# Second attention of a two-layer decoder: TensorE's order of rounds is pinned, the values products move to the third and fourth quarter, and gemm steps move to both ends

## The chip, the cores and the metric

The kernel runs on one core of one Trainium2 chip. The metric is the device time of one execution of the whole program, in microseconds; the times below are of several runs. One more execution was recorded by the hardware profiler, and every row of a trace shown here is from that one.

## What is computed

The reference is a decoder trunk of two layers on 512 tokens of 1024 channels, in float32. Each layer mixes tokens in two ways in parallel and then applies an MLP:

```python
h = rmsnorm(x, norm_mix)
proj = h @ w_in
q_a, k_a, v_a, f_a, q_b, kv_b, g_b, gate_a, gate_b = jnp.split(proj, ...)
...
o_a = fox_attention(...)                       # first attention: 8 heads, forget gate
y_a = from_heads(o_a) @ w_o_fox
...
o_c, o_s, o_w = nsa_attention(...)             # second attention: compressed, selected, window
o_n = g[..., 0:1] * o_c + g[..., 1:2] * o_s + g[..., 2:3] * o_w
y_b = from_heads(o_n.reshape(...)) @ w_o_nsa
mixed = jax.nn.sigmoid(gate_a) * y_a + jax.nn.sigmoid(gate_b) * y_b
x = x + mixed @ w_out
h = rmsnorm(x, norm_mlp)
x = x + jnp.square(jax.nn.relu(h @ w_up)) @ w_down
```

The second attention has 8 heads of 64 channels on 2 key and value heads. Its selected branch chooses up to 16 blocks of 64 keys; a sequence of 512 tokens has only 8, so that branch attends to all earlier tokens through its own keys and values. The window of 512 covers them too. Both branches are thus plain causal attention with keys of their own; the compressed branch has 31 pooled keys.

## The kernel before

**Products.** A float32 product is three matmuls on operands split into a high and a low half: `gemm` (L219 to L221) issues high weight by high input, high by low, low by high for each block of 128 channels. A weight tile arrives as `raw` by a DMA on SP's queue; `convert` makes the halves, `wh` by a cast on ScalarE (L189) and `wl` by a subtraction on VectorE (L190). One conversion covers one weight tile of 128 x 1024. A *gemm step* is what `gemm` issues between two `yield`s: two blocks, six matmuls of 512 columns into the PSUM bank `ps_mm`. A whole projection is four steps.

**The second attention.** It is `attend_pairs`, called once per layer with eight pairs. Pair 2p is the selected branch (kind 0) of heads 2p and 2p+1, pair 2p+1 the window branch of the same two heads. In round t the loop interleaves the scores of pair t, the values of pair t-1 and gemm steps; there are rounds 0 to 8, the last with values only. A round has four quarters. The tuples of the plan say how many steps of the scores and of the values generator go into each quarter.

- `pair_scores` takes the query rows in blocks of 128, last block first (i = 3, 2, 1, 0). For each it makes scores (L590) in one of two PSUM banks `ps_S`, the row maximum on VectorE (`softmax_part`, L542, output `mx`), the exponential on ScalarE (L543), and after every second block the normalised halves on ScalarE (L560) and VectorE (L561). Those go to SP's queue as a DMA that transposes them into PT (L611). Block 0 is made for a pair and its mate at once from the shared keys `kk`, so only pairs of kind 0 have it: a *kk pair*, two scores groups of 256 columns.
- `pair_values` multiplies PT with the values (L623) in five steps: three products on the blocks of rows 3 and 2, then two on the rest. At the last step of a window pair `after` adds the compressed branch (L1065) and makes the head outputs, `oh` on ScalarE (L1073) and `o` on VectorE (L1074).

**The gemm steps beside it.** The generator `fill2` hands out 88 steps: the gate projections (`gate_tanh`, L1096), the half products of the first attention's output with `wo` (`half`, summed by `ma`, L1106), the last two query projections, and beside two of these the compressed scores (`cmp_gen`): six matmuls (L792 to L794), a copy on ScalarE (L796), four transposes (L800), a softmax in small steps. `lead` steps go ahead of round 0, `NSA_FILL` are owed in each quarter of rounds 0 to 7, `LAST_FILL` in each quarter of round 8, and `run(fill)` issues what is left. Behind that come the half products of the second attention's output with `wo` and the weight tiles of the MLP, whose first sums on VectorE are at L1518 (from `raw` of `wup`) and whose halves ScalarE makes at L1536 (`sh`).

**What sets the order.** The code's order is what the program emits; a scheduler then orders each engine's instructions by its own estimate of when operands are there, as long as dependencies hold. `high_priority(20)` in `softmax_part` lets maxima and exponentials go ahead of what was emitted shortly before. The first attention ahead of it (`attend`) runs eight *fox* units in the same manner, with transposes on TensorE (L463).

Of the kernel before, what the change touches and what calls it, by code (L numbers as in the profile page):

```python
# [137 lines left out]
def run(*gens):  # L138
    for g in gens:
        for _ in g:  # L140
            pass


class Body:
# [469 lines left out]
    def pair_values(self, P):  # L614
# [22 lines left out]
        for w, (o, b) in enumerate(((X, 1), (Y, 3))):  # L637
            product(parts(o)[:, :, 128:], b, 8, slice(w, w + 1))
            if not first:
                P["after"](w)  # L640

    def attend_pairs(self, pairs, fill, rate, lead):

        n = len(pairs)
        owed = 0.0
        for _ in range(lead):
            next(fill)
        self.PP = self.EE.bitcast(F16).rearrange("p a (b k) -> p (a b) k", k=128)
        for t in range(n + 1):
            plan = []  # L650
            if t < n:
                while not pairs[t]["ready"]():
                    next(fill)
                plan.append((self.pair_scores(pairs[t]), (2, 2, 2, 2) if pairs[t]["kind"] == 0 else (2, 2, 2, 0)))
            if t:
                plan.append((self.pair_values(pairs[t - 1]), (0, 2, 1, 2)))
            for k in range(4):
                for g, at in plan:
                    for _ in range(at[k]):
                        next(g, None)  # L660
                if k == 3:
                    for g, _ in plan:
                        for _ in g:
                            raise AssertionError
                owed += rate if t < n else self.LAST_FILL
                while owed >= 1.0:
                    owed -= 1.0
                    next(fill, None)
        run(fill)

    def compress(self, kc, vc, small, l):
# [275 lines left out]
    def layer(self, l, u):  # L947
# [55 lines left out]
        def proj(i, key, fn, tag="mm"):  # L1003
            def done(ps):
                st[key] = fn(ps)
            return self.block(wb[i], u, done, tag)
# [27 lines left out]
        def qproj(p):  # L1034
            return proj(12 + p, ("qb", p), lambda ps: self.q_pair(self.roped(ps)))

        def cmp_gen(hk):
            yield from self.cmp_probs(hk)
# [19 lines left out]
        def nsa_pairs(p):  # L1058
            hk, f = divmod(p, 2)
            O = []  # L1060

            def after(side):
                ps, q = O[side], slice(256 * side, 256 * side + 256)
                for e in range(2):
                    nc.tensor.matmul(ps[:, 256 * e:256 * e + 256], self.vz[:, hk, e], self.pc[hk][f][:, q],  # L1065
                                     start=False, stop=True, skip_group_check=True)
                if side == 0:
                    st["ob", p] = self.t("tmp2", [128, T], name="o")
                o = st["ob", p]
                t = self.t("tmp", [128, 256], name="oh")  # L1070
                for e in range(2):
                    s, x, c = slice(64 * e, 64 * e + 64), slice(64 * (1 - e), 64 * (1 - e) + 64), slice(256 * e, 256 * e + 256)
                    nc.scalar.activation(t[s], ps[x, c], AF.Copy, scale=self.sc[x, 2:3])  # L1073
                    nc.vector.scalar_tensor_tensor(o[s, q], ps[s, c], self.sc[s, 2:3], t[s], op0=OP.mult, op1=OP.add)  # L1074
                if side == 1:
                    st["ob", p] = self.out_pair(o)

            q = lambda e: st["qb", p][:, e]
            gate = lambda br: lambda rows: gt[:, rows, br, 2 * p:2 * p + 2].rearrange("p b h -> p h b")
            b_ = dict(kind=1, ready=lambda: hk in self.pc, q=q, k=lambda: st["kw"][:, hk], O=O,  # L1080
                      v=lambda b: VN[:, b, 2 + hk], gate=gate(2), after=after)
            a_ = dict(kind=0, ready=lambda: ("qb", p) in st and "kw" in st, q=q, k=lambda: st["ks"][:, hk], O=O,
                      v=lambda b: VN[:, b, hk], gate=gate(1), mate=b_,
                      kk=lambda: self.kk[:, :, hk].rearrange("p f b t -> p f (b t)"))
            return [a_, b_]
# [8 lines left out]
        def gate_tanh(ps, tag="tmp"):  # L1094
            s = self.t(tag, [128, T], name="gate")
            nc.vector.tensor_mul(s, ps, R)  # L1096
            nc.scalar.activation(s, s, AF.Tanh, scale=0.5)
            return s

        def gated(m0):  # L1100
            for m in (m0, m0 + 1):
                yield from proj(16 + m, ("ga", m), gate_tanh)
            w = self.weights(a["wo"][l, 0, m0 // 2].rearrange("p i c -> p (i c)"))
            for m in (m0, m0 + 1):
                yield from half(0, m, w)
                nc.vector.scalar_tensor_tensor(MA[m // 2][:, m % 2], st["ga", m], 1.0, st["y"],  # L1106
                                               op0=OP.add, op1=OP.mult)

        def fill2():
            yield from beside(cmp_gen(0), gated(0))  # L1110
            yield from qproj(2)
            yield from gated(2)
            yield from qproj(3)
            yield from beside(cmp_gen(1), gated(4))
            yield from gated(6)
            for m in range(8):
                yield from proj(24 + m, ("gb", m), lambda ps: gate_tanh(ps, ("oh", "ol")[m % 2]))

        self.attend_pairs([u for p in range(4) for u in nsa_pairs(p)], fill2(), self.NSA_FILL, 2)
        yb = [st["ob", p] for p in range(4)]  # L1120


# [10 lines left out]
        for m in range(8):  # L1133
# [3 lines left out]
            t, y = st["gb", m], MA[m // 2][:, m % 2]  # L1137
# [117 lines left out]
            yield next(g)  # L1255

    FOX_FILL = 1.8
    NSA_FILL = 2.15
    LAST_FILL = 4.0
    BUFS.update(tmp2=1)  # L1260

    WARM = 8
# [700 lines left out]
def beside(a, b):  # L1963

    for _ in b:
        next(a, None)
        yield
    yield from a
# [30 lines left out]
```

## Time and profile before

| what | value |
|---|---|
| median of 3 runs | 1465.31 us (1463.86 to 1468.54) |
| profiled execution, its own time | 1464.53 us |
| its span in the trace | 1462.8 us |
| mean granted TensorE clock | 0.994 of full speed |
| TensorE busy | 1424.8 us (97%) |
| VectorE busy | 1192.2 us (82%) |
| ScalarE busy | 928.8 us (63%) |
| GpSimd busy | 142.3 us (10%) |

The span is what the trace covers; the execution takes 1.7 us more around it. The busy time of TensorE counts each matmul from its start to its modelled end. In layer 0 the second attention and what surrounds it lie between about 160 and 350 us of the span, in layer 1 between about 880 and 1072 us.

### The profile page before, as it was taken

How to read it: one execution, taken by the hardware profiler on the slowest of the kernel's cores; microseconds unless marked ns; L12 is line 12 of the kernel's file. 1: busy time of each engine (PE TensorE's matmuls, PEld its weight loads, DVE VectorE, ACT ScalarE, POOL GpSimd, SP SyncE). 2: the span in 40 equal slices, each digit the busy share in tenths (PEclk: the TensorE clock that was granted, in tenths of full speed). 3: DMA queues.
4: the chain of work that ended last, by engine and by line, in shares of the span. 5: the costliest groups of instructions: out<-in, count | busy, mean ns of one | idle time of the engine just before them, and what ended most of it. 6: DMA issues, size and time to landing. Idle time of an engine off the chain costs nothing.

```text
span 1462.8 us, 22967 instructions
## 1 busy us (share of the span) xinstructions
PE 1424.8 (97%) x7948; PEld 1211.1 (83%) x7948; DVE 1192.2 (82%) x2490; ACT 928.8 (63%) x1939; POOL 142.3 (10%) x195
## 2 busy tenths in 40 slices
PE   9999998999999999999999999999999999999997
PEld 8877776767898999989888787766778989999896
DVE  6587888776789898989866878787587888989898
ACT  6375566773577584848454755777546775757485
POOL 2000100000011111111300011000000111111112
PEclk9999999999999999999999999999999999999999
DMA  7564567465447676777946645656743575867684
GB/s 255 167 158 137 141 150 163 115 154 177 137 129 195 174 176 163 196 171 194 273 135 166 180 117 141 140 135 142 192 121 101 145 174 143 192 173 183 159 216 115
DMA packets 163955, 237.66 MB, mean 162 GB/s; under 512 B 94592, under 2 KB 94976, under 8 KB 163840
## 3 DMA queue, kind: packets, MB, share of 16 engines
q1 hardware_dynamic: 143440, 184.80, 42.8%
q0 software_dynamic: 17664, 46.67, 18.4%
q10 hardware_dynamic: 2736, 4.74, 0.9%
q8 instruction: 62, 1.02, 0.3%
q14 instruction: 53, 0.43, 0.1%
HBM read 168.46 MB, written 6.29 MB: 119 GB/s over the span
## 4 chain that ended last, share of the span: by engine, by line
PE 80%; DMA 7%; DVE 7%; ACT 3%; issue 2%; SPq 0%; POOL 0%; ACTq 0%; DVEq 0%; POOLq 0%
PE ps_mm L1710 7%; PE ps_S L1710 7%; PE ps_mm L219 7%; PE ps_mm L220 7%; PE ps_mm L221 7%; PE ps_S L1583 6%; PE ps_PT L1583 6%; PE ps_mm L1583 5%; DMA PT<-EE 4%; PE ps_O L1710 3%; PE ps_PT L1710 3%; PE ps_O L1583 3%; DMA raw<-wup 2%; DVE EE L561 2%; PE ps_S L590 1%
## 5 line engine op out<-in xcount | busy, mean ns | idle before, releaser
L219 PE MATMUL ps_mm<-uh,wh 128*128 128x512 f32 x480 | 195.1, 406 | 0.4 <-DVE ma L1106 0.3
L220 PE MATMUL ps_mm<-ul,wh 128*128 128x512 f32 x480 | 190.9, 398 | 0.0
L221 PE MATMUL ps_mm<-uh,wl 128*128 128x512 f32 x480 | 189.0, 394 | 0.0
L189 ACT CAST wh<-raw 128x1024 fp32r<-128x1024 f32 (+2 forms) x111 | 112.6, 1015 | 103.1 <-PE ps_mm L220 64.7
L190 DVE TENSOR_TENSOR wl<-raw,wh 128x1024 fp32r<-128x1024 f32 (+2 forms) x111 | 130.6, 1177 | 23.8 <-ACT wh L189 23.6
L1692 ACT CAST sh<-raw 128x512 fp32r<-128x512 f32 x160 | 96.8, 619 | 77.7 <-DVE raw L1791 26.7
L1700 DVE TENSOR_TENSOR sl<-raw,sh 128x512 fp32r<-128x512 f32 x160 | 106.3, 685 | 18.8 <-ACT sh L1692 18.8
L219 PEld LDWEIGHTS ps_mm<-uh,wh 128*128 128x128 f32 x480 | 90.6, 189 | 20.1 <-issue 1.9
L221 PEld LDWEIGHTS ps_mm<-uh,wl 128*128 128x128 f32 x480 | 90.5, 188 | 17.0
L220 PEld LDWEIGHTS ps_mm<-ul,wh 128*128 128x128 f32 x480 | 90.8, 189 | 16.3
L1557 POOL DMA_DIRECT2D raw<-raw x32 | 28.0, 875 | 694.4 <-DVE sl L1550 465.7
L543 ACT ACTIVATE E<-E,mx 128x512 f32<-128x512 f32 (+3 forms) x112 | 64.7, 579 | 37.9 <-DVE mx L542 29.8
L1550 DVE TENSOR_TENSOR sl<-raw,sh 128x512 fp32r<-128x512 f32 x128 | 83.9, 685 | 5.1 <-ACT sh L1536 4.0
L1583 PE MATMUL ps_S<-t,sh 128*128 128x256 f32 x384 | 83.3, 282 | 0.2
L561 DVE SCALAR_TENSOR_TENSOR EE<-E,rr,EE 128x384 f16<-128x384 f32 (+2 forms) x144 | 63.0, 494 | 19.4 <-ACT EE L560 19.4
L1536 ACT CAST sh<-raw 128x512 fp32r<-128x512 f32 x128 | 75.2, 617 | 4.4 <-DVE sl L1700 3.7
L1536 ACT CAST sh<-sx 128x512 fp32r<-128x512 f32 x96 | 58.2, 614 | 26.2 <-DVE sx L1518 24.4
L1550 DVE TENSOR_TENSOR sl<-sx,sh 128x512 fp32r<-128x512 f32 x96 | 64.5, 686 | 11.6 <-ACT sh L1536 11.6
L1583 PE MATMUL ps_S<-t,sl 128*128 128x256 f32 x256 | 71.9, 281 | 0.0
L219 PE MATMUL ps_mm<-oh,wh 128*128 128x512 f32 x160 | 63.6, 398 | 6.5 <-DVE gate L1096 4.8
L542 DVE CUSTOM_DVE_ANT_0 E<-ps_S,ct 128x512 f32<-128x512 f32 (+3 forms) x112 | 55.0, 512 | 16.7 <-PE ps_S L590 15.4
L560 ACT ACTIVATE EE<-E,rr 128x384 f16<-128x384 f32 (+2 forms) x144 | 63.0, 508 | 8.8 <-ACT E L543 4.0
(467 smaller groups left out, 4346.0 us busy)
## 6 DMA issues: line engine op xcount, KB each, us to landing
raw<-wb SPq DMA_DIRECT2D x64, 512.0 KB
raw<-wup SPq DMA_DIRECT2D x64, 512.0 KB
raw<-wt POOLq DMA_DIRECT2D x48, 512.0 KB, 6.9
raw<-wt SPq DMA_DIRECT2D x32, 512.0 KB
sx<-wt SPq DMA_DIRECT2D x64, 256.0 KB
kd<-hl SPq DMA_DIRECT2D x40, 256.0 KB
w<-w SPq DMA_DIRECT2D x32, 256.0 KB
raw<-wo SPq DMA_DIRECT2D x16, 512.0 KB
```

The lines of the kernel that those rows point to most:

```text
L189: nc.scalar.copy(h[:, :n], raw[:, :n])
L190: nc.vector.tensor_tensor(lo[:, :n], raw[:, :n], h[:, :n].bitcast(F32), op=OP.subtract)
L219: mm(ps, h[:, c], xh, start=start and i == 0, stop=False)
L220: mm(ps, h[:, c], xl, start=False, stop=False)
L221: mm(ps, lo[:, c], xh, start=False, stop=stop and i == ks - 1)
L561: self.nc.vector.scalar_tensor_tensor(out[1], x, f, out[0], op0=OP.mult, op1=OP.subtract)
L1536: self.nc.scalar.copy(h, self.source(k, i))
L1550: self.nc.vector.tensor_tensor(lo, self.source(k, i), h.bitcast(F32), op=OP.subtract)
L1583: self.nc.tensor.matmul(ps, w, x, skip_group_check=True, **kw)
L1692: self.nc.scalar.copy(h, self.operand(d, i, p))
L1700: self.nc.vector.tensor_tensor(lo, self.operand(d, i, p), h.bitcast(F32), op=OP.subtract)
L1710: self.nc.tensor.matmul(ps[t][:, cols], a[:, s], m, start=new and f == 0, stop=f == 2, skip_group_check=True)
```

## The change

A new function `in_order` chains TensorE's instructions, each to the one emitted before it, so that the scheduler keeps their order. The chain goes from round 1 (`mark` is taken there once that round's plan is made) to the end of the loop; the rest behind the loop is left free. It adds no wait on the chip by itself, since an engine's own instructions run in order. The values' steps move from quarters 2, 3 and 4 (2, 1, 2) to quarters 3 and 4 (3, 2). Six steps instead of two go ahead of round 0, 2.0 instead of 2.15 are owed in a quarter, 3.0 instead of 4.0 in one of the last round. The 88 steps, 2 + 68 + 16 + 2 before (ahead, in rounds 0 to 7, in round 8, behind), are 6 + 64 + 12 + 6 after it.

```diff
--- before.py
+++ after.py
@@ -639,6 +639,17 @@
             if not first:
                 P["after"](w)
 
+    def in_order(self, first, engines):
+
+        last = {}
+        for i in self.nc.cur_bb.bb.instructions[first:]:
+            if i.engine not in engines:
+                continue
+            if i.engine in last:
+                self.tc.add_manual_dep(i, last[i.engine].name, mybir.DependencyInfo(
+                    mybir.DependencyClass.NoSync, mybir.DependencyReason.DATA), reason="order")
+            last[i.engine] = i
+
     def attend_pairs(self, pairs, fill, rate, lead):
 
         n = len(pairs)
@@ -653,7 +664,9 @@
                     next(fill)
                 plan.append((self.pair_scores(pairs[t]), (2, 2, 2, 2) if pairs[t]["kind"] == 0 else (2, 2, 2, 0)))
             if t:
-                plan.append((self.pair_values(pairs[t - 1]), (0, 2, 1, 2)))
+                plan.append((self.pair_values(pairs[t - 1]), (0, 0, 3, 2)))
+            if t == 1:
+                mark = len(self.nc.cur_bb.bb.instructions)
             for k in range(4):
                 for g, at in plan:
                     for _ in range(at[k]):
@@ -666,6 +679,7 @@
                 while owed >= 1.0:
                     owed -= 1.0
                     next(fill, None)
+        self.in_order(mark, (mybir.EngineType.PE,))
         run(fill)
 
     def compress(self, kc, vc, small, l):
@@ -1116,7 +1130,7 @@
             for m in range(8):
                 yield from proj(24 + m, ("gb", m), lambda ps: gate_tanh(ps, ("oh", "ol")[m % 2]))
 
-        self.attend_pairs([u for p in range(4) for u in nsa_pairs(p)], fill2(), self.NSA_FILL, 2)
+        self.attend_pairs([u for p in range(4) for u in nsa_pairs(p)], fill2(), self.NSA_FILL, 6)
         yb = [st["ob", p] for p in range(4)]
 
 
@@ -1255,8 +1269,8 @@
             yield next(g)
 
     FOX_FILL = 1.8
-    NSA_FILL = 2.15
-    LAST_FILL = 4.0
+    NSA_FILL = 2.0
+    LAST_FILL = 3.0
     BUFS.update(tmp2=1)
 
     WARM = 8
```

**The start of the scores.** The listing is TensorE's order in layer 0 where the first scores come (`ps_S` from keys `kd` and queries `q2`). The matmuls of L463 are transposes of the last fox units; `ps_mm` from `uh`, `ul` and a weight half are gemm steps. Before:

```order
L219 MATMUL ps_mm_1900<-uh_177,wh_1766 128x512
L463 MATMUL ps_PT_1842<-ct_184,EE_635 128x128
L220 MATMUL ps_mm_1900<-ul_178,wh_1766 128x512
L221 MATMUL ps_mm_1900<-uh_177,wl_1767 128x512
L219 MATMUL ps_mm_1900<-uh_225,wh_1766 128x512
L590 MATMUL ps_S_1945<-kd_1588,q2_1754 128x512 x2
L463 MATMUL ps_PT_1842<-ct_184,EE_635 128x128
```

After (L814 are the transposes of the compressed scores, L800 before):

```order
L814 MATMUL ps_PT_1922<-ct_184,tmp_1920 128x128 x4
L220 MATMUL ps_mm_1956<-ul_124,wh_1907 128x512
L221 MATMUL ps_mm_1956<-uh_123,wl_1908 128x512
L219 MATMUL ps_mm_1956<-uh_168,wh_1907 128x512
L220 MATMUL ps_mm_1956<-ul_169,wh_1907 128x512
L221 MATMUL ps_mm_1956<-uh_168,wl_1908 128x512
L219 MATMUL ps_mm_1956<-uh_177,wh_1907 128x512
L220 MATMUL ps_mm_1956<-ul_178,wh_1907 128x512
L221 MATMUL ps_mm_1956<-uh_177,wl_1908 128x512
L590 MATMUL ps_S_1997<-kd_1588,q2_1754 128x512 x2
L590 MATMUL ps_S_2003<-kd_1588,q2_1754 128x512 x2
L219 MATMUL ps_mm_1956<-uh_225,wh_1907 128x512
```

The fox transposes and the compressed scores, which stood behind the first scores matmul, now stand ahead of it, with more gemm matmuls.

**Round 2 on TensorE.** The listing is TensorE's order where the kk pair of round 2 comes. Before, within a gate projection:

```order
L219 MATMUL ps_mm_2521<-uh_273,wh_2417 128x512
L220 MATMUL ps_mm_2521<-ul_274,wh_2417 128x512
L590 MATMUL ps_S_2423<-kk_900,q2_1824 128x256 x2
L221 MATMUL ps_mm_2521<-uh_273,wl_2418 128x512
L590 MATMUL ps_S_2433<-kk_900,q2_1824 128x256 x2
L623 LDWEIGHTS vn_482
L623 MATMUL ps_O_2567<-PT_2365,vn_482 128x512
```

After (`oh` and `ol` here are the halves of the first attention's output, the operand of a half product):

```order
L220 MATMUL ps_mm_2430<-ol_1839,wh_2313 128x512
L221 MATMUL ps_mm_2430<-oh_1838,wl_2314 128x512
L219 MATMUL ps_mm_2430<-oh_1892,wh_2313 128x512
L220 MATMUL ps_mm_2430<-ol_1893,wh_2313 128x512
L221 MATMUL ps_mm_2430<-oh_1892,wl_2314 128x512
L590 MATMUL ps_S_2443<-kk_900,q2_1824 128x256 x2
L590 MATMUL ps_S_2453<-kk_900,q2_1824 128x256 x2
L623 LDWEIGHTS vn_482
L623 MATMUL ps_O_2277<-PT_2273,vn_482 128x512
```

The kk pair now stands right behind the last matmul of a half product, with nothing between its two groups.

**Round 2 on VectorE.** The same place on VectorE; L542 with output `mx` is a row maximum that empties a scores bank. Before:

```order
L1106 SCALAR_TENSOR_TENSOR ma_1897<-gate_2407,ps_mm_2489 128x512
L561 SCALAR_TENSOR_TENSOR EE_635<-E_2302,rr_2299,EE_635 128x3x128
L561 SCALAR_TENSOR_TENSOR EE_635<-E_2303,rr_2299,EE_635 128x3x128
L1074 SCALAR_TENSOR_TENSOR o_2463<-ps_O_2185,sc_741,oh_2464 64x256
L1074 SCALAR_TENSOR_TENSOR o_2463<-ps_O_2186,sc_741,oh_2473 64x256
L190 TENSOR_TENSOR wl_2529<-raw_2421,wh_2528 128x1024
L542 ISA E_2300,mx_2390<-ps_S_2387,ct_184 128x256
L542 ISA mx_2390 128x1
L542 ISA E_2301,mx_2396<-ps_S_2393,ct_184 128x256
```

After (`ma` is on L1120):

```order
L561 SCALAR_TENSOR_TENSOR EE_635<-E_2331,rr_2327,EE_635 128x3x128
L1120 SCALAR_TENSOR_TENSOR ma_1897<-gate_2389,ps_mm_2430 128x512
L190 TENSOR_TENSOR wl_2511<-raw_2403,wh_2510 128x1024
L542 ISA E_2328,mx_2414<-ps_S_2411,ct_184 128x256
L542 ISA mx_2414 128x1
L542 ISA E_2329,mx_2420<-ps_S_2417,ct_184 128x256
L542 ISA mx_2420 128x1
L542 ISA E_2328,mx_2446<-ps_S_2443,ct_184 128x128
```

The two maxima of 256 columns, which free the banks that the kk pair is written to, stand directly behind `ma` of that same half product and the conversion `wl_2511`; before, `ma` stood five instructions ahead of the conversion.

## Rows read from the trace of the kernel before

**Rows 1.** Waits of TensorE, 160 to 352 us, layer 0.

```profile
engine line waited for: us in total, times, longest us
PE ps_O L623 <- DMA PT<-EE: 5.9, 14, 1.2
PE ps_S L590 <- issue: 3.6, 1, 3.6
PE ps_mm L219 <- DVE gate L1096: 2.9, 2, 1.9
PE ps_S L590 <- DVE mx L542: 0.8, 1, 0.8
PE ps_mm L219 <- ACT sh L1536: 0.4, 1, 0.4
...
```

**Rows 2.** Waits of TensorE, 880 to 1072 us, layer 1.

```profile
PE ps_O L623 <- DMA PT<-EE: 4.0, 10, 1.0
PE ps_S L590 <- issue: 2.9, 1, 2.9
PE ps_mm L219 <- DVE gate L1096: 1.9, 1, 1.9
PE ps_mm L219 <- ACT sh L1536: 1.3, 1, 1.3
PE ps_O L623 <- DVE mx L542: 1.2, 2, 0.7
PE ps_S L590 <- DVE mx L542: 0.7, 1, 0.7
...
```

**Rows 3.** Timeline of TensorE: start us, us, instruction, [idle before, releaser].

```profile
162.05 0.39 PE L221 MATMUL ps_mm<-uh,wl 128*128 128x512 f32 x1
162.28 0.40 PE L219 MATMUL ps_mm<-uh,wh 128*128 128x512 f32 x1
166.32 1.19 PE L590 MATMUL ps_S<-kd,q 128*128 128x512 f32 x2 [3.65 <-issue]
...
252.92 0.50 PE L219 MATMUL ps_mm<-oh,wh 128*128 128x512 f32 x1 [1.86 <-DVE gate L1096]
...
301.93 0.50 PE L590 MATMUL ps_S<-kk,q 128*128 128x256 f32 x2 [0.75 <-DVE mx L542]
...
889.02 0.70 PE L590 MATMUL ps_S<-kd,q 128*128 128x512 f32 x2 [2.87 <-issue]
```

**Rows 4.** Windows: us, busy of each engine, granted clock (PEclk), DMA.

```profile
core 0: us, PE busy (x) PEld busy (x) DVE busy (x) ACT busy (x) POOL busy (x), PEclk, DMA share, GB/s
160.00:350.00 190.00, 175.42 (x807) 133.35 (x806) 143.95 (x360) 123.83 (x290) 2.26 (x3) 0.99 0.61 153
166.00:170.00 4.00, 3.68 (x13) 3.04 (x14) 0.33 (x1) 0.95 (x2) 0.00 (x0) 0.57 1.01 222
252.00:254.00 2.00, 1.08 (x5) 0.90 (x6) 2.00 (x4) 1.10 (x2) 0.00 (x0) 1.00 0.58 115
890.00:894.00 4.00, 4.00 (x16) 3.21 (x16) 1.75 (x3) 0.97 (x2) 0.00 (x0) 0.60 0.79 183
```

**Rows 5.** VectorE's instructions by form, 190 to 310 us: busy us, mean ns | idle before.

```profile
L190 DVE TENSOR_TENSOR wl<-raw,wh 128x1024 fp32r<-128x1024 f32 x13 | 15.9, 1221 | 3.3 <-ACT wh L189 3.2
...
L542 DVE CUSTOM_DVE_ANT_0 E<-ps_S,ct 128x256 f32<-128x256 f32 x14 | 5.3, 418 | 0.0
```

**Rows 6.** ScalarE's instructions by form, 190 to 310 us.

```profile
L560 ACT ACTIVATE EE<-E,rr 128x384 f16<-128x384 f32 x24 | 13.9, 604 | 2.7 <-ACT E L543 1.5 <-issue 1.2
L189 ACT CAST wh<-raw 128x1024 fp32r<-128x1024 f32 x13 | 13.6, 1049 | 6.1 <-PE ps_mm L220 5.9
...
L560 ACT ACTIVATE EE<-E,rr 128x128 f16<-128x128 f32 x20 | 7.4, 388 | 1.2 <-DMA PT<-EE 1.2
L543 ACT ACTIVATE E<-E,mx 128x384 f32<-128x384 f32 x12 | 7.3, 610 | 4.7 <-DVE mx L542 4.7
...
L796 ACT COPY tmp<-ps_S 128x512 f32<-128x512 f32 x1 | 0.6, 566 | 0.0
```

**Rows 7.** Timeline of VectorE.

```profile
301.44 0.42 DVE L542 CUSTOM_DVE_ANT_0 E<-ps_S,ct 128x256 f32<-128x256 f32 x1
...
339.37 0.69 DVE L1518 TENSOR_TENSOR sx<-raw 128x512 f32<-128x512 f32 x1 [5.08 <-DMA raw<-wup]
```

## Prediction

> **What bounds the kernel now.** I read the page first: TensorE is busy nearly everywhere, so time is won only where it stands still or runs at half clock. Second, the waits of TensorE in the stretch that the diff touches, from the last fox units to the first products with `wo`, once per layer. In layer 0 the five longest kinds make 13.6 us in 19 waits [rows 1], in layer 1 the six longest 12.0 us in 16 [rows 2]. They are of three sorts: one wait ahead of the first scores matmul, put down to issue; 14 and 10 short ones of the values matmuls for the transposed probabilities PT; and a few behind VectorE or ScalarE (a bank that has not been emptied, a late conversion).
>
> Third, the timeline says what a wait costs beyond its figure. A streaming matmul of 512 columns starts 0.23 us after the one before (162.05, 162.28), but is shown 0.39 us long; a wait is counted from that shown end. So each loses 0.16 us more than its row says [rows 3]: 19 x 0.16 = 3.0 us and 16 x 0.16 = 2.6 us.
>
> Fourth, the start of the scores. TensorE waits 3.65 us in layer 0 and 2.87 us in layer 1 [rows 3], and the granted clock is 0.57 over 166 to 170 us and 0.60 over 890 to 894 us, that is the lower level (1.2 GHz) for most of both stretches [rows 4]. Lost by that: 3.7 x 0.43 = 1.6 us (the matmuls begin at 166.32), and 4 x 0.40 = 1.6 us. Behind the wait of 1.86 us that ended at 252.92 [rows 3] the clock is 1.00 [rows 4].
>
> So what the stretch can give back at most is 13.6 + 3.0 + 1.6 = 18.2 us in layer 0 and 12.0 + 2.6 + 1.6 = 16.2 us in layer 1, together 34.4 us. The matmuls themselves are the same before and after, so the forecast is this sum less the waits that the new order makes.
>
> **The six steps ahead.** Four more gemm steps, 24 matmuls at 0.23 us = 5.5 us, and the drain of the fox units that stood behind the stalled matmul, now run before the first scores. TensorE left off at about 162.5 and q was there at 166.3 [rows 3], 3.8 us later, less than the 5.5 us. I take this wait and its clock loss as gone. Not all of it is won: transposes of the last fox unit now come up at once, and two early scores matmuls meet VectorE still in the six-step cmp chain. I take 1.2 us for these, from the small waits of rows 1 and 2 (0.4 to 1.3 us); the bounds are 0 and 3.65.
>
> **Values in quarters three and four.** PT of the first group is asked for a quarter of a round later: 12 gemm matmuls (2.7 us) plus the scores of that quarter, against waits of at most 1.2 us [rows 1]. I take all 24 PT waits as gone. What would uncover them is a PT that comes more than 3 us later than now; its transposes stand in SP's queue behind fewer weight fetches in some rounds and the same in others, so I leave 0.
>
> **The pinned order, which adds waits.** Scores use two banks. The pinned list runs four scores matmuls, 12 gemm matmuls, four scores, and so on; before, up to 20 gemm matmuls stood ahead of a late one. The second and third order listings give the price at round 2. The first kk pair needs the bank whose row maximum VectorE now takes behind `ma` of the half product and behind the conversion `wl_2511`, and TensorE has nothing between that half product and kk. Count from T, the start of the last half matmul. The last reader of the old `wh` ends at T - 0.23 + 0.39 = T + 0.16; ScalarE's cast takes 1.05 us [rows 6], VectorE's subtraction 1.22, the 256-wide maximum 0.42 [rows 5], and 0.07 passes to the matmul (301.44 + 0.42 [rows 7] to 301.93 [rows 3]), with 0.04 at each hand-over between. That is T + 2.96 against T + 0.23: 2.7 us lost. `ma` itself (0.69, the length of a 128x512 step [rows 7]) lies beside the cast.
>
> Round 4 has `ma` but no conversion ahead of the maximum: 0.43 + 0.69 + 0.42 + 0.07 - 0.23 = 1.4 us. In round 6 the half products come two quarters earlier and the maximum stands behind neither: 0.
>
> Round 0 is not pinned, yet its kk pairs now stand right ahead of the pinned scores of round 1. From the second 384-wide maximum on, the chain is exp 0.61, two small steps 0.3, a cast that ScalarE has ahead of the halves 1.05, four casts of 384 and two of 128 (2.4 + 0.8), a last 384-wide half on VectorE of about the same 0.6, and the maximum 0.42 [rows 5, 6]: 6.2 us, against 12 matmuls = 2.8 us on TensorE. That is 3.4 us, and about 0.9 more because round 1's scores need the banks of both kk pairs emptied, each by two maxima no longer than 0.42. Together 4.3.
>
> Round 3: the six cmp matmuls are followed at once by transposes of their copy. ScalarE's copy takes 0.57 [rows 6]: 0.39 + 0.57 + 0.11 - 0.23 = 0.85 us.
>
> **The six steps behind.** 54 matmuls (12.3 us) instead of 36 now lie between the last values and the first `wo` product. In layer 0 VectorE waits until 339.37 for `wup` with the head outputs queued behind it [rows 7], and the waits for ScalarE's `sh` and for the gate come from there [rows 1, 2]. With 4 us more cover I take them as gone, but the last gate weights are now converted behind that same wait, so I leave 0.5 us.
>
> **The clock behind the new stops.** Stops of 3.4 and 2.7 us are idle for about 3.2 and 2.5 us. The rows show the drop behind 2.87 and none behind 1.86, so these lie near and between. I take half of one drop, 0.9 us a layer; the bounds are 0 and 1.6 x 2. The Trainium skill, TensorE: Matmul & The Clock Gate, section "A second HAM failure mode: psum-queue depth-cycling", says that a TensorE which pauses briefly between groups while it cycles through PSUM banks loses clock again and again; by it every bank stop here would pay. The trace bears that out only for the longer two of three waits.
>
> **The sum.** New losses a layer: 1.2 + 4.3 + 2.7 + 0.85 + 1.4 + 0.5 + 0.9 = 11.9 us, 23.8 for two. Gain 34.4 - 23.8 = 10.6 us. The profiled execution took 1464.53 us, which gives 1453.9; the median of the runs is 0.8 us above it, so 1454.7, say 1454.5.
>
> **Rivals.** *The stops cost little.* VectorE, busy 143.95 of 190 us in the stretch [rows 4], may come to the maxima earlier than my chain says, since it no longer waits with TensorE for q. With half of 11.9 the gain is 34.4 - 11.9 = 22.5: 1443. For it: TensorE waited for a maximum only 0.8 and 1.9 us before [rows 1, 2]. Against it: at round 2 the order of VectorE, not its load, makes the wait. Chance 0.16.
>
> *The clock falls at each bank stop.* Rounds 0, 2, 3 and 4 would each pay 1.6 us instead of 0.9 in all: 2 x (6.4 - 0.9) = 11 us more, which leaves a gain of about 0: 1465. The 1.00 behind 1.86 us [rows 4] speaks against it. The Trainium skill, TensorE: Matmul & The Clock Gate, speaks for it. With the smaller misses that end there, 0.14.
>
> *Slower: TensorE, bound to the list, waits for VectorE in every round with kk.* Now it can run gemm steps while softmax is late; pinned it cannot, and the waits pass on from one round to the next. If rounds 0, 2, 4 and 6 each stop 4.3 us with a clock loss of 1.6, a layer loses 4 x 5.9 + 2.5 = 26 us against 17.2: 2 x 8.9 = 18 us slower, 1483. It decides from 2.1 us a round with the clock loss, 3.7 us without. For it: round 0 reaches that by my chain. Against it: rounds 4 and 6 do not. Chance 0.08.
>
> *The start wait only moves.* If q lands later because SP meets more fetches ahead of it, 5 us a layer come back and the whole gain is gone; but both q groups stand at the same place of SP's queue as before. This is in the 0.14.
>
> **Numbers.** The forecast holds 0.62 (gain 4.4 to 18 us). Within 0.3% is 4.4 us either way, about what a measurement can tell from no change. Faster 0.62 + 0.16 - 0.01 = 0.77, same 0.15, slower 0.08. The range: up to half of the stops gone (1443, a little below it 1442), and down to a gain of 2 us (1463), which leaves about 0.2 outside.
>
> **What would show it.** In the changed kernel's waits the row of issue ahead of L590 should be gone in both layers, and the clock 1.00 there; the values' waits for PT near 0; new waits of L590 for `mx` of 2 to 3.5 us at kk of rounds 0 and 2 and 1.2 at round 4; a wait of a transpose for `tmp` below 1 us. The prediction is wrong if PT waits stay, if kk waits are above 4 us in more than one round of a layer, or if the first `wo` product comes to wait for its gate longer than before.

## The result, and the profile after

The changed kernel takes 1476.11 us (median of 5 runs, 1473.08 to 1478.55) against 1464.38 us for the kernel before (now also 5 runs); the ratio is 1.0075, 95% interval 1.0055 to 1.0095. It is slower by 11.7 us where about 10 us faster was forecast, and outside the forecast's range of 1442 to 1463 us. The profiled execution spans 1474.3 us (1462.8 before), with a mean granted clock of 0.984 (0.994).

The time is lost in the two second attentions. Two marks that both kernels have show it: a matmul in the first attention that reads `G`, and the first product with `wout` in bank PT. TensorE's timeline of the kernel before has them, in layer 0, at:

```profile
137.77 0.62 PE L753 MATMUL ps_S<-G,small 128*128 128x64 f32 x4
...
379.56 0.39 PE L219 MATMUL ps_PT<-oh,wh 128*128 128x512 f32 x1
```

TensorE's timeline of the changed kernel, layer 0, with the marks and the longer stops between them:

```profile
136.98 0.50 PE L767 MATMUL ps_S<-G,small 128*128 128x64 f32 x3
...
187.52 0.80 PE L590 MATMUL ps_S<-kk,q 128*128 128x256 f32 x4 [3.02 <-issue]
...
220.29 0.85 PE L590 MATMUL ps_S<-kk,q 128*128 128x256 f32 x4 [2.51 <-DVE mx L542]
...
236.59 0.80 PE L806 MATMUL ps_S<-qs,kcz 128*128 128x512 f32 x1 [4.91 <-ACT qs L357]
...
239.24 1.12 PE L814 MATMUL ps_PT<-ct,tmp 128*128 128x128 f32 x4 [0.68 <-ACT tmp L810]
...
264.69 0.80 PE L590 MATMUL ps_S<-kk,q 128*128 128x256 f32 x4 [1.17 <-issue]
...
343.75 0.77 PE L219 MATMUL ps_mm<-uh,wh 128*128 128x512 f32 x1 [4.21 <-DVE gate L1110]
...
384.51 0.39 PE L219 MATMUL ps_PT<-oh,wh 128*128 128x512 f32 x1
```

From mark to mark 241.8 us became 247.5, 5.7 us more; in layer 1 it is 6.4 (861.30 to 1104.12 before, 866.29 to 1115.48 after). The first scores start without a wait, so the 3.65 us of [rows 3] are gone. In their place stand stops at kk, at the compressed scores (L806) and at a gate projection behind the last values. The waits of TensorE in the changed kernel, layer 0, and under the line of dots the two longest of layer 1:

```profile
PE ps_S L806 <- ACT qs L357: 4.9, 1, 4.9
PE ps_mm L219 <- DVE gate L1110: 4.2, 1, 4.2
PE ps_S L590 <- issue: 4.2, 2, 3.0
PE ps_S L590 <- DVE mx L542: 3.0, 2, 2.5
PE ps_PT L814 <- ACT tmp L810: 0.7, 1, 0.7
...
PE ps_S L806 <- ACT qs L357: 4.8, 1, 4.8
PE ps_mm L219 <- DVE gate L1110: 4.7, 1, 4.7
```

The values' waits for PT of [rows 1, 2] are all gone: no row of L623 is left. But 17.3 us in 8 waits (a last one of 0.3 us is not shown) stand where 13.6 us in 19 stood. These fewer and longer stops cost more than their sum, for the granted clock falls behind most of the long ones. Windows of the changed kernel behind the start, the 3.02 us stop, the 2.51, the 4.91 and the 4.21 (columns as in [rows 4], the clock third from the end):

```profile
170.00:176.00 6.00, 6.00 (x29) 4.95 (x28) 5.91 (x13) 3.26 (x6) 0.00 (x0) 1.00 0.41 132
...
188.00:192.00 4.00, 3.68 (x10) 2.73 (x11) 2.70 (x15) 3.54 (x15) 0.00 (x0) 0.60 1.24 138
220.00:224.00 4.00, 3.71 (x22) 3.02 (x23) 2.36 (x16) 3.68 (x15) 0.00 (x0) 1.00 1.17 124
236.00:244.00 8.00, 6.73 (x20) 4.70 (x21) 3.98 (x9) 1.90 (x5) 0.00 (x0) 0.57 0.76 155
343.00:349.00 6.00, 5.25 (x12) 4.18 (x13) 4.11 (x6) 3.95 (x6) 1.60 (x2) 0.50 0.49 157
```

The clock is 1.00 at the start, where [rows 4] had 0.57, and behind the stop of 2.51; behind the three longer ones it is at the lower level (1.2 GHz) most of the time. For the time that TensorE is busy there, that costs 3.68 x 0.40 = 1.5, 6.73 x 0.43 = 2.9 and 5.25 x 0.50 = 2.6 us.

What is late at the two longest stops stands on VectorE, and at the first of them on ScalarE too. The timeline of VectorE in the changed kernel, ahead of the compressed scores, with ScalarE's two lines of the same time, and then VectorE's ahead of the gate:

```profile
231.94 1.20 DVE L190 TENSOR_TENSOR wl<-raw,wh 128x1024 fp32r<-128x1024 f32 x1
...
233.13 0.69 DVE L343 TENSOR_TENSOR tmp<-tmp 128x512 f32<-128x512 f32 x1
233.95 2.74 DVE L561 SCALAR_TENSOR_TENSOR EE<-E,rr,EE 128x384 f16<-128x384 f32 x6
236.61 0.68 DVE L358 SCALAR_TENSOR_TENSOR qs<-tmp,qs 128x512 fp32r<-128x512 f32 x1
...
233.30 2.72 ACT L560 ACTIVATE EE<-E,rr 128x384 f16<-128x384 f32 x6 [1.69 <-issue]
235.93 0.61 ACT L357 ACTIVATE qs<-tmp 128x512 fp32r<-128x512 f32 x1
...
337.28 0.69 DVE L1532 TENSOR_TENSOR sx<-raw 128x512 f32<-128x512 f32 x1 [9.24 <-DMA raw<-wup]
...
338.61 1.90 DVE L1088 SCALAR_TENSOR_TENSOR o<-ps_O,sc,oh 64x256 f32<-64x256 f32 x4
341.08 1.23 DVE L190 TENSOR_TENSOR wl<-raw,wh 128x1024 fp32r<-128x1024 f32 x1 [0.56 <-ACT wh L189]
...
342.92 1.29 DVE L1110 TENSOR_TENSOR gate<-ps_mm,R 128x512 f32<-128x512 f32 x2
```

In round 3 each engine makes one half of the query, `qs`, behind six normalised halves of 384 columns (ScalarE L357, which ends TensorE's wait, and VectorE L358); on VectorE a conversion stands ahead of these too. In the tail VectorE stands 9.24 us at `wup`, and the gate that empties the bank of `ps_mm` comes 5.6 us after that.

### The profile page after: what moved, and what is told of

Its sections match the earlier page's. It is cut to its first block, busy times and chain, and to the rows that moved or that the text cites. A ratio compares the mean times of both kernels' runs of the same rounds, so it can differ in the third digit from the quotient of the medians.

```text
span 1474.3 us, 22974 instructions
## 1 busy us (share of the span) xinstructions
PE 1428.9 (97%) x7948; PEld 1221.3 (83%) x7948; DVE 1194.9 (81%) x2490; ACT 931.2 (63%) x1939; POOL 141.9 (10%) x195
## 3 DMA queue, kind: packets, MB, share of 16 engines
q0 software_dynamic: 17664, 46.67, 18.2%
## 5 line engine op out<-in xcount | busy, mean ns | idle before, releaser
L221 PE MATMUL ps_mm<-uh,wl 128*128 128x512 f32 x480 | 192.0, 400 | 0.0
L1564 DVE TENSOR_TENSOR sl<-sx,sh 128x512 fp32r<-128x512 f32 x96 | 64.6, 685 | 13.6 <-ACT sh L1550 13.6
L561 DVE SCALAR_TENSOR_TENSOR EE<-E,rr,EE 128x384 f16<-128x384 f32 (+2 forms) x144 | 62.3, 495 | 12.4 <-ACT EE L560 11.7
L542 DVE CUSTOM_DVE_ANT_0 E<-ps_S,ct 128x512 f32<-128x512 f32 (+3 forms) x112 | 54.9, 513 | 12.4 <-PE ps_S L590 11.2
L1597 PEld LDWEIGHTS ps_S<-t,sh 128*128 128x128 f32 x384 | 63.5, 189 | 1.0 <-ACT yz L1649 1.0
```

The costliest lines, as they stand in the source:

```text
L221: mm(ps, lo[:, c], xh, start=False, stop=stop and i == ks - 1)
L1564: self.nc.vector.tensor_tensor(lo, self.source(k, i), h.bitcast(F32), op=OP.subtract)
L1597: self.nc.tensor.matmul(ps, w, x, skip_group_check=True, **kw)
```

## The experiments

| run | edit | median us | against before, 95% |
|---|---|---|---|
| changed kernel | | 1476.11 | 1.0055 to 1.0095 |
| e1_tail | two steps behind | 1465.29 | 0.9999 to 1.0024 |
| e2_cmp | compressed scores four steps later | 1473.77 | 1.0051 to 1.0093 |
| e3_nopin | no chain | 1475.15 | 1.0067 to 1.0101 |
| e4_lead | before, six steps ahead | 1464.39 | 0.9992 to 1.0015 |
| e5_tailcmp | e1 and e2 | 1464.19 | 0.9983 to 1.0008 |
| e6_tailkk | e1, kk in banks PT | 1454.86 | 0.9926 to 0.9951 |
| e7_all3 | e6 and e2 | 1454.56 | 0.9924 to 0.9951 |
| e8_leadkk | e4, kk in banks PT | 1464.51 | 0.9991 to 1.0011 |
| e9_kknopin | e6, no chain | 1459.37 | 0.9957 to 0.9981 |
| e10_kkcmp2 | e6, compressed scores two steps later | 1447.39 | 0.9866 to 0.9895 |
| e11_kkq | e10, query halves with priority | 1453.97 | 0.9918 to 0.9941 |
| e12_oldq | e10, old quarters | 1448.68 | 0.9872 to 0.9909 |

The kernel before, run beside them on the same chip, had medians of 1463.8 to 1464.9.

**e1_tail**, on the changed kernel:

```diff
-    LAST_FILL = 3.0
+    LAST_FILL = 4.0
```

> The changed kernel with LAST_FILL 4.0 again, so that two gemm steps instead of six stand behind the last values. Theory A: of the 11.7 us that the change cost, the tail is one half: TensorE stops 4.2 us (layer 0) and 4.7 us (layer 1) there for a bank that VectorE empties only behind its wait for wup, and then runs about 5 us at the lower clock. With 18 matmuls more ahead of the last values the stop is gone: about 7.1 us back in layer 0 and 7.2 in layer 1, less the 1.8 and 3.6 us that the kernel before lost at the same place, so about 1467 us (1463 to 1471), and no wait of L219 for the gate above 2 us. Rival B: the tail is bound by the arrival of wup, and the stop only moves to the first wo product: 1474 to 1477, with a wait of 4 us there.

1465.29: theory A, 10.8 us back where 8.9 was expected (10.2 if each run is taken against the kernel before that ran beside it). The six steps behind the values are nearly the whole of the 11.7 us. The waits of TensorE in this run have one short row for the gate in layer 0 and in layer 1:

```profile
PE ps_mm L219 <- DVE gate L1110: 0.5, 1, 0.5
...
PE ps_mm L219 <- DVE gate L1110: 1.0, 2, 0.8
```

**e2_cmp**, on the changed kernel:

```diff
-            yield from beside(cmp_gen(1), gated(4))
+            g4 = gated(4)
+            yield from self.first(g4, 4)
+            yield from beside(cmp_gen(1), g4)
```

> The changed kernel, with the compressed scores of the second key head started four gemm steps later (behind the first gate projection instead of with its first step). Theory A: the stop of 4.9 us in round 3 is the wait for the halves of the fourth query projection, emitted three matmul groups before; four steps (24 matmuls, 5.5 us) cover it, and the slow clock behind it goes too: 4.9 + 3.4 and 4.8 + 4.0 us less, about 1459 us (1456 to 1464). Rival B: it is ScalarE's and VectorE's queue in round 3 that is late, so that the next scores matmul stops in place of the compressed one: 1468 to 1476, with a new wait for mx of 3 us or more in round 3.

1473.77, theory B by the time, and not told apart from the changed kernel. The wait for `qs` is gone, but its successors take its place, in round 4 and not in round 3 as B had it: the transposes wait 1.9 us for the copy instead of 0.7, and in TensorE's timeline the kk pair of round 4 stops 3.39 us where it stopped 1.17:

```profile
259.35 1.20 PE L590 MATMUL ps_S<-kk,q 128*128 128x256 f32 x4 [3.39 <-issue]
```

**e5_tailcmp**, both edits:

> The changed kernel with LAST_FILL 4.0 and the late compressed scores together. Theory A, by which stops add up: 1465.3 (the tail alone undone), less 2 x (4.8 + 0.7 + 3.0) of round 3, plus the 1.9 of the copy that the late scores showed: about 1452 us. Theory B, by which VectorE's order of work sets when the next row maximum comes and a stop that is taken away comes back at the next scores: with the late scores the kk pair of round 4 stopped 3.4 us instead of 1.2 and ran on at the lower clock, so that rounds 3 and 4 together lost 11 us as before: 1462 to 1466 us.

1464.19, theory B again: beside the tail alone the late compressed scores bring 1.1 us, with intervals that overlap. A stop that is removed comes back at the next scores.

**e3_nopin**, on the changed kernel:

```diff
-        self.in_order(mark, (mybir.EngineType.PE,))
```

> The changed kernel without the chain on TensorE's order; all else as changed. Theory A: the bank stops of rounds 0, 2, 3 and 4 come from the chain and vanish; the tail stays; start and PT waits stay gone: 1464.4 - 10.5 - 13.7 + 8.9 = 1449 us (1446 to 1454). Rival B: it is the chain that removed the PT waits, and without it the scheduler draws the values forward to where PT is not there: the PT waits of the kernel before come back, 1464.4 - 10.5 + 8.9 = 1463 us (1459 to 1466).

1475.15, outside both. B's mechanism holds: the waits for PT are back (4.8 us in 15 waits in layer 0, 7.7 in 14 in layer 1), though the values are in the new quarters. What B missed is the tail, which stops TensorE here as well (5.7 us in layer 0 and 4.4 in layer 1, 4.2 and 4.7 with the chain), and a kk stop in round 6 of 3.2 us. Taking the chain away alone thus brings nothing back: it trades its stops for others.

**e4_lead**, on the kernel before:

```diff
-        self.attend_pairs([...], fill2(), self.NSA_FILL, 2)
+        self.attend_pairs([...], fill2(), self.NSA_FILL, 6)
...
-    NSA_FILL = 2.15
+    NSA_FILL = 2.0
```

> The kernel before, with six gemm steps instead of two ahead of round 0 and 2.0 instead of 2.15 owed in a quarter (6 + 64 + 16 + 2 steps), nothing else. Theory A: the wait ahead of the first scores and its slow clock are gone in both layers: 3.65 + 2.87 + 2 x 0.16 + 2 x 1.6 = 10 us less, 1454 us (1452 to 1458). Rival B: q is only asked for later, or VectorE's six-step chain becomes the wait at the first scores: 1461 to 1466, with a wait of L590 above 2 us in the first rounds.

1464.39, no change. It is not B's wait at the first scores: these start at clock 1.00 without a wait. TensorE's timeline in this run, the two marks of above and one stop:

```profile
137.22 0.62 PE L753 MATMUL ps_S<-G,small 128*128 128x64 f32 x4
...
299.00 1.22 PE L590 MATMUL ps_S<-kk,q 128*128 128x256 f32 x4 [3.30 <-DVE mx L542]
...
379.52 0.39 PE L219 MATMUL ps_PT<-oh,wh 128*128 128x512 f32 x1
```

242.3 us from mark to mark, as before (241.8). What the start won is given back: the kk wait of round 6, 0.75 us in [rows 3], is 3.30 us, and the clock from 299 to 303 us is 0.50, where the kernel before had 1.00 behind its 0.75.

**e6_tailkk**, on e1:

```diff
-                ps = self.p("S")
+                ps = self.p("S" if i else "PT")
```

> The changed kernel with LAST_FILL 4.0, and the scores of the kk pairs written to the PSUM banks PT, which the second attention uses only for the compressed scores, so that they need not wait for a row maximum. Theory A: the stops of 3.0, 2.5 and 1.2 us at kk and their slow clock (6, 4 and 1.7 us a layer in all) are gone: 1465.3 - 2 x 11 = 1443 us. Theory B: the scores behind kk need the same banks of S, whose maxima VectorE still takes behind its halves and conversions, so that most of a stop moves there: 1458 to 1465, with waits of 2 us or more at kd.

1454.86, between the two: 10.4 us better than e1. The stops of rounds 2 and 4 are gone; that of rounds 0 and 1 moved to the kd scores behind and is 2.5 us there instead of 3.0, with small ones of up to 1.2 us at later kd scores. The wait for `qs` is now 5.3 us:

```profile
PE ps_S L806 <- ACT qs L357: 5.3, 1, 5.3
PE ps_S L590 <- DVE mx L542: 4.8, 5, 2.5
...
```

**e7_all3**, e6 with the edit of e2:

> The changed kernel with LAST_FILL 4.0, the late compressed scores and the kk pairs in the banks PT. Theory A: all stops that the chain made are gone but the copy: 1465.3 - 22 - 13 = 1430 us. Theory B: 1452 to 1463; the gain over the run with kk alone is then below 5 us.

1454.56, no gain over e6: B, by a wait that I made. The second transposes of the compressed scores hold a bank PT until VectorE has made `cp`, and four steps late they meet the kk pair of round 4:

```profile
PE ps_PT L590 <- DVE cp L844: 4.3, 1, 4.3
```

**e8_leadkk**, e4 with the edit of e6:

> The kernel before with six steps ahead (2.0 owed in a quarter) and the kk pairs in the banks PT; no chain, values in the old quarters. Theory A: what the six steps won at the start (5.3 us a layer) was given back by the kk stop of round 6 (3.3 us and as much by the clock, against 0.8 before); with the bank free the gain stands: 1453 to 1457 us. Theory B: the region is as long as VectorE's and ScalarE's chain of softmax steps, which the six steps do not move: 1462 to 1465 us, with PT waits in place of the kk wait.

1464.51, B. With the bank free the stop of round 6 sits at the kd scores behind (2.76 us for a maximum), and in layer 1 the waits for PT grow to 8.8 us.

**e9_kknopin**, e6 without the chain:

> The run with LAST_FILL 4.0 and the kk pairs in the banks PT (1454.9 us), without the chain on TensorE's order. Theory A: the chain keeps the values behind the point where PT is there; without it the scheduler draws them forward, the PT waits come back (4.8 and 7.7 us in the run of the changed kernel without the chain) and the gain goes: 1463 to 1466. Theory B: the third and fourth quarter and the free banks do it, the chain is not needed: 1453 to 1457.

1459.37, between. The waits for PT are back, as A says, but the loss is 4.5 us, not the whole gain. In layer 0 and layer 1:

```profile
PE ps_O L623 <- DMA PT<-EE: 5.4, 11, 1.3
...
PE ps_O L623 <- DMA PT<-EE: 7.5, 11, 2.1
```

**e10_kkcmp2**, e6 with the edit of e2, but `self.first(g4, 2)`:

> The run with LAST_FILL 4.0 and the kk pairs in the banks PT (1454.9 us), and the second compressed scores two gemm steps later instead of four. Theory A: the wait for the query halves falls from 5.3 by the 2.7 us of twelve matmuls, with 1 to 2 us of slow clock, and the compressed scores are through before kk of round 4 wants the bank PT (the run with four steps waited 4.3 us there): 1454.9 - 2 x 4 = 1447 us. Theory B: it moves on to round 4 again: 1453 to 1456, with a wait of 2 us or more at kk of round 4.

1447.39, theory A by the time. The compressed scores wait 3.3 us where they waited 5.3 (2.7 less was expected), and for a maximum instead of `qs`; the kk pair of round 4 waits for nothing, and the copy is 0.7 again. The longest waits of TensorE in layer 0:

```profile
PE ps_S L590 <- DVE mx L542: 4.2, 4, 2.5
PE ps_S L806 <- DVE mx L542: 3.3, 1, 3.3
...
PE ps_PT L814 <- ACT tmp L810: 0.7, 1, 0.7
```

With e12, which is not told apart from it, this is the fastest version, 1.2% below the kernel before and 1.9% below the changed one.

**e11_kkq**, on e10 (priority for the third and fourth query projection's rotation and halves):

```diff
-            return proj(12 + p, ("qb", p), lambda ps: self.q_pair(self.roped(ps)))
+            def q(ps):
+                if p < 2:
+                    return self.q_pair(self.roped(ps))
+                with self.tc.high_priority(60):
+                    return self.q_pair(self.roped(ps))
+            return proj(12 + p, ("qb", p), q)
```

> As the run with two steps, and the rotation and halves of the third and fourth query projection get priority 60 ahead of the scheduler's order, so that ScalarE and VectorE make them before the twelve normalised halves (2.7 us on each) instead of behind. Theory A: the stop ahead of the compressed scores goes whole, with its slow clock: 1454.9 - 2 x 7 = 1441 us. Theory B: the normalised halves now come later, PT with them, and values or maxima wait in turn: 1450 to 1456.

1453.97, B: 6.6 us worse than e10. The compressed scores wait only 0.9 us, but the maxima that were pushed back stop the scores for 7.7 us in four waits in layer 0 (4.2 in e10) and 9.2 in layer 1.

**e12_oldq**, on e10:

```diff
-                plan.append((self.pair_values(pairs[t - 1]), (0, 0, 3, 2)))
+                plan.append((self.pair_values(pairs[t - 1]), (0, 2, 1, 2)))
```

> The fastest run so far (1447.4 us: chain, six steps ahead, LAST_FILL 4.0, kk in the banks PT, compressed scores two steps later) with the values in the old quarters, (0, 2, 1, 2) instead of (0, 0, 3, 2). Theory A: the chain alone does not hide PT; pinned in the second quarter the values find PT as late as in the kernel before, with nothing to fill the wait: 5 to 8 us a layer back, 1457 to 1463. Theory B: what hides PT is that the chain keeps all gemm matmuls of the quarter ahead of the values, whichever quarter it is: 1446 to 1450, PT waits below 2 us a layer.

1448.68, B: not told apart from e10. No wait of L623 stands among TensorE's waits of this run, in layer 0 or 1; the longest of layer 0 are:

```profile
PE ps_S L590 <- DVE mx L542: 3.6, 2, 2.4
PE ps_S L806 <- DVE mx L542: 3.6, 1, 3.6
...
```

## Why the prediction was wrong, step by step

- **The six steps ahead.** Right for the place: wait and slow clock are gone, with none of the 1.2 us left for small waits. Counted as won for the kernel it is wrong where it stands alone (e4, e8): TensorE then arrives earlier at VectorE's maxima and stops there.
- **Values in quarters three and four.** The waits for PT went, as forecast, but the cause was misplaced. With the new quarters and no chain they stay (e3, e9); with the chain and the old quarters they are gone (e12). So the chain does it. That it works by keeping each quarter's gemm matmuls ahead of its values is my reading and was not tested by itself; that its stops elsewhere give PT the time has this against it: in layer 0 of e12 TensorE has no stop from 240 to 298 us, and no wait for PT there either.
- **The pinned order.** The walk through VectorE's order held: with the 0.16 us that the prediction counts for each wait, round 0 to 1 cost 3.02 + 0.32 + 2 x 0.16 = 3.7 us (4.3 forecast), round 2 2.51 + 0.16 = 2.7 (2.7), round 4 1.17 + 0.16 = 1.3 (1.4), the copy in round 3 0.68 + 0.16 = 0.84 (0.85).
- **Round 3, the step that failed first.** It counted the copy behind the compressed scores and not what they read. The pinned list puts them one gemm step (six matmuls) behind the query projection, whose halves VectorE and ScalarE make behind the softmax halves: stops of 4.9 and 4.8 us, with 2.9 us (above) and 5.47 x 0.49 = 2.7 us of clock (967 to 974 us, granted 0.51). Removing it alone brought 2.3 and 1.1 us (e2, e5), neither told apart from nothing, since the kk stop of round 4 then grew; with kk in another bank two steps of delay brought 7.5 us (e6 to e10).
- **The six steps behind, the step that failed most.** It said 0.5 us a layer; e1 gives 10.8 us for both. I counted the time up to the first `wo` product and the weights' conversion, not the bank. Behind the last values the 54 matmuls are a quarter of a projection and two whole ones. The second whole one needs the bank that the quarter filled, so TensorE stops after 30 of the 54, at 339.5 us; VectorE, which empties that bank, is held by `wup` until 337.28 us and by head outputs and a conversion until 342.92. The stop is at a gate projection ahead of the first `wo` product, where none of the prediction's signs of being wrong looked.
- **The clock.** 0.9 us a layer was forecast. By the windows above three stops of layer 0 cost 1.5 + 2.9 + 2.6 = 7.0 us. The rival of a clock that falls at each bank stop is partly right: in the changed kernel's profile it fell behind each stop above 3 us and behind one of 2.51 in layer 1 (0.57 from 950 to 954 us), not behind that of 2.51 in layer 0. Its price was looked for behind too few waits. The kernel before pays it in two more places of layer 1, behind stops of 0.3 to 1.3 us (rows in the last section): 3.53 x 0.43 = 1.5 and 4.00 x 0.43 = 1.7 us, 3.2 us that the 16.2 us of that layer leave out. The Trainium skill, TensorE: Matmul & The Clock Gate, section "A second HAM failure mode: psum-queue depth-cycling", tells of short idles between matmul groups that make the clock go back and forth. The traces agree in some places and not in others, the kernel before included.

Put together for layer 0: the stops make 17.3 us, the 0.16 of eight waits 1.3 and the clock 7.0, together 25.6. Of the kernel before, the 18.2 that could be won and two short waits that the prediction left out (0.3 and 0.2 us, with 0.16 each) make 19.0. That is 6.6 us worse; the marks say 5.7. The difference is not settled. The slower rival (TensorE stopped by VectorE in every round with kk) gave the right side for the wrong place: the stops of the rounds alone leave it at 1465 (e1).

## What to carry to other kernels

Pinning TensorE's order traded many short waits for a few long ones here, and most of these cost their clock too; follow every operand of a pinned instruction, what it reads and the bank it writes, back through the order of the engine that releases it. Where stops are made by one engine's order, removing one can let the next grow (e2, e5, e7); what helped here was to cut the dependence itself (another PSUM bank, with the chain: e6, not e8) and then to retime (e10). Work put behind a loop is cover only as far as the engine that empties its banks is not waiting for something else.

## What was not expected of the hardware

The same stop can cost the clock or not. The kk stop of 3.02 us near 188 us stands in several runs; over 188 to 192 us the granted clock was 0.60 in the changed kernel and 0.50 in e1, and in e2, whose timeline and window have

```profile
187.88 0.80 PE L590 MATMUL ps_S<-kk,q 128*128 128x256 f32 x4 [3.02 <-issue]
```

```profile
188.00:192.00 4.00, 3.68 (x17) 2.89 (x18) 2.78 (x17) 3.86 (x16) 0.00 (x0) 1.00 1.34 139
```

it was 1.00. So a single profile can show a stop near 3 us at either price. What decides it stays open; the scatter of the run times does not tell, for e2 ran from 1468.2 to 1478.2 us and e6, which has stops of 5.3 and 2.5 us, from 1454.6 to 1457.0.

Nor does it take one long stop. TensorE's timeline of the kernel before, layer 1, has three short stops close together and, 43 us later, two:

```profile
1024.05 0.50 PE L590 MATMUL ps_S<-kk,q 128*128 128x256 f32 x2 [0.71 <-DVE mx L542]
1025.51 0.38 PE L623 MATMUL ps_O<-PT,vn 128*128 128x512 f16 x1 [0.96 <-DMA PT<-EE]
...
1026.82 0.59 PE L623 MATMUL ps_O<-PT,vn 128*128 128x512 f16 x1 [0.47 <-DVE mx L542]
...
1069.17 0.47 PE L219 MATMUL ps_mm<-oh,wh 128*128 128x512 f32 x1 [1.29 <-ACT sh L1536]
...
1070.21 0.50 PE L221 MATMUL ps_mm<-oh,wl 128*128 128x512 f32 x1 [0.34 <-DVE wl L190]
```

The granted clock behind both is 0.57; behind the same three stops in layer 0 (0.75, 0.96 and 0.46 us) it is 1.00:

```profile
1026.00:1030.00 4.00, 3.53 (x12) 2.25 (x11) 2.33 (x10) 3.29 (x13) 0.00 (x0) 0.57 0.36 72
1070.50:1074.50 4.00, 4.00 (x12) 3.09 (x12) 4.00 (x7) 2.84 (x5) 1.84 (x2) 0.57 0.79 200
302.00:306.00 4.00, 2.58 (x12) 1.65 (x13) 3.46 (x15) 3.95 (x16) 0.00 (x0) 1.00 0.83 157
```
